# Clamped decay differences as Relu on ScalarE, and a convolution from an SBUF copy, in a hybrid decoder layer

## The chip, the cores and the metric

The kernel runs on one core of one Trainium2 chip. The metric is device time in microseconds (us) from the first to the last instruction of one execution; times of a kernel are the median of several executions. Engines are called by the names of the profile: PE (TensorE matmul) with PEld (its weight loads), DVE (VectorE), ACT (ScalarE), POOL (GpSimd), SP (SyncE, which only issues transfers here). L529 is line 529 of the kernel.

## What is computed

One decoder layer over 1024 tokens of width 1024, float32. One input projection (width 4696) feeds two mixers: group A, a Mamba-2 state-space part (16 heads of 64, two B/C groups of state 128), and group B, a sparse attention in which every query keeps its 256 best keys by a small indexer. Their outputs are projected, added to the input, and normalized; a convolved SwiGLU channel mixer and a second normalization follow. The change touches group A alone, of which this is the core:

```python
xbc = jax.nn.silu(_causal_dwconv(xbc, ssd_conv_w, ssd_conv_b))   # width 4, 1536 channels
xs, bm, cm = jnp.split(xbc, [SSD_INNER, SSD_INNER + SSD_BC], axis=-1)
dt = jax.nn.softplus(dt_raw + dt_bias)
acs = jnp.cumsum((dt * a).reshape(bsz, nc, q, SSD_GROUPS, hg), axis=2)   # in chunks of 128
seg = acs[:, :, :, None] - acs[:, :, None, :]
lmat = jnp.exp(jnp.where(causal[:, :, None, None], seg, -jnp.inf))
y_diag = jnp.einsum("bclsg,bclsgh,bcsghp->bclghp", cb, lmat, xdt)
```

## The kernel before, in words

**Matrix products.** Each float32 operand is split in a high and a low part (`split`, L125 to L130: the low part is a subtraction, on POOL for the weights of this stage), and each product is three matmuls (`three`, L156 to L159). `cols_half` (L161) makes 128 output channels by 512 tokens with 24 matmuls into one PSUM bank of tag "ip", which has two banks. `tok_proj_gen` (L603) makes 128 tokens by 256 columns of the gate z or of v into the same two banks and evicts them on ACT (L617).

**Convolution.** `conv_tile(j)` (L469) makes one of twelve tiles of 128 channels of x (j below 8), B (8, 9) and C (10, 11), tokens along the free axis. It goes by halves of 512 tokens. ACT reads the half from PSUM, scaled by the last tap and with the bias (L479); the other three taps are multiply-adds on DVE that read PSUM shifted (L483). The first three tokens of the second half need the end of the first: ACT keeps three columns in `edge` (L478), and three narrow multiply-adds use them (L486). All of this stands under a raised priority (EV_PRIO). After the second half comes SiLU on ACT (L491, L494), and for x eight transposes on PE and copies on ACT (L500, L502). The tile has a buffer of tag "wo" (8 buffers, shared with the indexer's scores) or "pt" (3).

**Chunked scan.** `ssd_gen(g)` (L512) walks eight chunks of 128 tokens for each of the two groups. Per chunk, SP loads a row of cumulative decays, broadcast over partitions, as `acsb` (L525, 512 KB in SBUF); eight DVE instructions, one per head, make min(row - own decay, 0) over 128x128 (L529); ACT takes the exponential of all eight (L531); DVE multiplies by the masked product of C and B (L535, L536); POOL makes the scaled inputs (L539 to L543). Then PE multiplies with the running state (L548) and makes its increment (L554) and the chunk's output (L564), and DVE adds the increment to the state (L558).

**Order.** SP's queue is in program order. The order on the other engines is set when the kernel is built, by a planner that simulates a time line and takes the ready instruction of highest priority. The program interleaves generators: the indexer's scores (`score_gen`) beside the first projections; then `topk_gen` (a search over 32 bits, with sign passes on ACT at L353, counts on DVE at L350 and some small integer operations such as L358, L364 and L367 after each) beside `main`: convolution tiles 0 to 3, then z, q and `ssd_gen(0)`, then tiles 9, 11, 4 to 7 and the gate of group 0, then z, v, q and `ssd_gen(1)`. `ssd_gen` has a priority of its own (SSD_PRIO) under EV_PRIO. The attention begins at about 640 us, the channel mixer after 1040 us. The channel mixer has a convolution of width 3 whose input lies in SBUF (L1058, L1061); the attention's exponentials are L686.

Of the kernel before, what the change touches and what calls it, by code (L numbers as in the profile page):

```python
# [12 lines left out]
AF = mybir.ActivationFunctionType  # L13
OP = mybir.AluOpType

P = 128
L = 1024
# [40 lines left out]
def hybrid_layer(ctx, tc, x, w_in, ssd_conv_w, ssd_conv_b, dt_bias, a_log, d_skip, ssd_norm_g,  # L58
                 idx_k_norm_g, idx_k_norm_b, w_out, ln1_g, ln1_b, w_up, ffn_conv_w, ffn_conv_b,
                 w_down, ln2_g, ln2_b, out):  # L60
    nc = tc.nc
# [15 lines left out]
    def big(name, dtype=F32, shape=(P, 1024), tag="t4"):  # L77
        return pool.tile(list(shape), dtype, name=name, tag=tag, bufs=BUFS[tag])

    def bank(name, tag, shape=(P, 512)):  # L80
        return psum.tile(list(shape), F32, name=name, tag=tag, bufs=PBUFS[tag])

    def small(name, shape, dtype=F32, bufs=2):
        return pool.tile(list(shape), dtype, name=name, tag=name, bufs=bufs)

    def mid(name, dtype=F32, shape=(P, 512), tag="s2"):
        return pool.tile(list(shape), dtype, name=name, tag=tag, bufs=S2 if tag == "s2" else EV)
# [73 lines left out]
    def cols_half(w, mov, half, tag="ip"):  # L161

        hi, lo, m = w
        ps = bank("proj", tag)
        for k in range(NK):
            three(ps[:m], hi[:, k, :m], lo[:, k, :m], mov[0](half, k), mov[1](half, k), k == 0, k == NK - 1)
        return ps
# [23 lines left out]
    cw = consts.tile([P, 68], F32, name="cw")  # L191
    ps = bank("cwps", "tp")
# [3 lines left out]
    for half in range(2):  # L196
        s = slice(half * 512, half * 512 + 512)
        for k in range(NK):
            ps = bank("xtp", "lg")
# [8 lines left out]
    for half in range(2):  # L208
        ps = cols_half(w_small, xt, half)
        nc.scalar.activation(sg[:88, half * 512:half * 512 + 512], ps[:88], AF.Copy)  # L210
    tok = big("tok", shape=(P, 1024))[:, :NB * 88].rearrange("p (b c) -> p b c", c=88)
    for g in range(2):
        ps = bank("sgp", "tp")
# [21 lines left out]
    for b in range(NB):  # L235
        nc.vector.tensor_scalar(kn[:, b, :64], tok[:, b, 16:80], mv8[:, b, 0:1], rs8[:, b:b + 1],
                                op0=OP.subtract, op1=OP.mult)
# [4 lines left out]
    for g in range(2):  # L242
        s = slice(g * 512, g * 512 + 512)
        ps = bank("kip", "tp")
# [189 lines left out]
    def next_w(ahead=1):  # L434
        load_ahead(1)
        w = ready.pop(0)
        load_ahead(ahead)
        return w
# [3 lines left out]
    for t in range(4):  # L442
        w = w_qi if t == 0 else next_w()
        a, c = big("qsa", F32R, tag="pp"), big("qsb", F32R, tag="pp")
        for half in range(2):
            s = slice(half * 512, half * 512 + 512)
            ps = cols_half(w, xt, half)
# [20 lines left out]

    def conv_tile(j):  # L469
        w = next_w()  # L470
        t = big("conv", tag="wo" if j < 8 else "pt")
        edge = small("edge", (P, 3))
        for half in range(2):
            o = half * 512
            ps = cols_half(w, xt, half)
            with tc.high_priority(EV_PRIO):
                if half == 0:
                    nc.scalar.activation(edge, ps[:, 509:512], AF.Copy)  # L478
                nc.scalar.activation(t[:, o:o + 512], ps, AF.Identity, bias=cw[:, 48 + j:49 + j],  # L479
                                     scale=cw[:, 36 + j:37 + j])  # L480
                for sft in (1, 2, 3):
                    tap = cw[:, (3 - sft) * 12 + j:(3 - sft) * 12 + j + 1]
                    nc.vector.scalar_tensor_tensor(t[:, o + sft:o + 512], ps[:, :512 - sft], tap, t[:, o + sft:o + 512],  # L483
                                                   op0=OP.mult, op1=OP.add)
                    if half == 1:
                        nc.vector.scalar_tensor_tensor(t[:, o:o + sft], edge[:, 3 - sft:], tap, t[:, o:o + sft],  # L486
                                                       op0=OP.mult, op1=OP.add)
            yield
        if j >= 8:
            bc[j] = t  # L490
            nc.scalar.activation(t, t, AF.Silu)  # L491
        else:
            g, jj = divmod(j, 4)
            nc.scalar.activation(t, t, AF.Silu)  # L494
            if jj == 0:
                xs[g] = [big("xs", shape=(P, 2, 512), tag="pp") for _ in range(4)]
            for c4 in range(2):
                ps = bank("xsp", "tp")
                for c in range(4):
                    nc.tensor.transpose(ps[:, c * P:(c + 1) * P], t[:, (c4 * 4 + c) * P:(c4 * 4 + c + 1) * P], ident)  # L500
                for c in range(2):
                    nc.scalar.activation(xs[g][c4 * 2 + c][:, :, jj * P:(jj + 1) * P],  # L502
                                         ps[:, c * 256:c * 256 + 256].rearrange("p (c n) -> p c n", c=2), AF.Copy)


    def heads(ap, g, c):
        return ap[:, c, g * 8:g * 8 + 8][:, :, None].to_broadcast([P, 8, 64])

    def hv(t):
        return t.rearrange("p (h n) -> p h n", h=8)  # L510

    def ssd_gen(g, tag):  # L512
        dt, acs, eacs, cd, dd = decays
        bt, ct = bc[8 + g], bc[10 + g]
        state = None
        for c in range(NB):
            cs = slice(c * P, (c + 1) * P)
            if c % 4 == 0:
                ps = bank("btp", "tp")
                for j in range(4):  # L520
                    nc.tensor.transpose(ps[:, j * P:(j + 1) * P], bt[:, (c + j) * P:(c + j + 1) * P], ident)
                btok = mid("btok", shape=(P, 4, P))
                nc.scalar.activation(btok, ps.rearrange("p (j n) -> p j n", j=4), AF.Copy)
            ab = big("acsb", tag=tag, shape=(P, 8, P))
            nc.sync.dma_start(ab, bass.AP(tensor=a_dr.tensor, offset=a_dr.offset + (c * 16 + g * 8) * P,  # L525
                                          ap=[[0, P], [P, 8], [1, P]]))
            lm = big("lmat", tag=tag, shape=(P, 8, P))
            for h in range(8):
                nc.vector.tensor_scalar(lm[:, h, :], ab[:, h, :], acs[:, c, g * 8 + h:g * 8 + h + 1], 0.0,  # L529
                                        op0=OP.subtract, op1=OP.min)  # L530
            nc.scalar.activation(lm, lm, AF.Exp)  # L531
            ps = bank("cbps", "tp")
            nc.tensor.matmul(ps[:, :P], bt[:, cs], ct[:, cs], start=True, stop=True)
            cb = small("cbm", (P, P))
            nc.vector.tensor_tensor(cb, ps[:, :P], tri, op=OP.mult)  # L535
            nc.vector.tensor_tensor(lm, lm, cb[:, None, :].to_broadcast([P, 8, P]), op=OP.mult)  # L536
            xc = xs[g][c // 2][:, c % 2, :]
            xd = [mid("xdt"), mid("xdd") if c < NB - 1 else None]
            nc.gpsimd.tensor_tensor(hv(xd[0]), hv(xc), heads(dt, g, c), op=OP.mult)  # L539
            if c < NB - 1:  # L540
                nc.gpsimd.tensor_tensor(hv(xd[1]), hv(xc), heads(dd, g, c), op=OP.mult)
            skip = mid("skip")
            nc.gpsimd.tensor_tensor(hv(skip), hv(xc), dsk[:, g * 8:g * 8 + 8][:, :, None].to_broadcast([P, 8, 64]),  # L543
                                    op=OP.mult)
            yield
            if c:
                po = bank("yoff", "lg")
                nc.tensor.matmul(po, ct[:, cs], state, start=True, stop=True)  # L548
                off = mid("off")
                nc.vector.tensor_tensor(hv(off), hv(po), heads(eacs, g, c), op=OP.mult)  # L550
                nc.gpsimd.tensor_tensor(skip, skip, off, op=OP.add)
            if c < NB - 1:
                pst = bank("stps", "lg")
                nc.tensor.matmul(pst, btok[:, c % 4, :], xd[1], start=True, stop=True)  # L554
                new = mid("state")
                if c:
                    nc.gpsimd.tensor_tensor(hv(new), hv(state), heads(cd, g, c), op=OP.mult)
                    nc.vector.tensor_tensor(new, new, pst, op=OP.add)  # L558
                else:
                    nc.vector.tensor_copy(new, pst)  # L560
                state = new
            py = bank("yps", "lg")
            for h in range(8):
                nc.tensor.matmul(py[:, h * 64:h * 64 + 64], lm[:, h, :], xd[0][:, h * 64:h * 64 + 64],  # L564
                                 start=True, stop=True)
            nc.vector.tensor_tensor(xc, py, skip, op=OP.add)
            yield
# [335 lines left out]
    ps = bank("fwps", "tp")  # L903
# [36 lines left out]
    for i, b in enumerate(LN_ORDER):  # L940
        bs = slice(b * P, (b + 1) * P)
        o = (b % 4) * P
# [8 lines left out]
        for n in range(2):  # L951
            ns = slice(n * 512, n * 512 + 512)
            ps = bank("ops", ("ip", "lg")[n])
# [7 lines left out]
        for k4 in range(2):  # L961
            ps = bank("hTp", "tp")
# [69 lines left out]
    for j in range(NF):  # L1032
# [10 lines left out]
        c = bank("pc", "tp")  # L1043
# [13 lines left out]
        for x_, v_, ct in ((xu, vu, NF + j), (xg, vg, j)):  # L1057
            nc.scalar.activation(v_, x_, AF.Identity, bias=fw[:, 132 + ct:133 + ct], scale=fw[:, 88 + ct:89 + ct])  # L1058
            for sft in (1, 2):
                tap = fw[:, (2 - sft) * 44 + ct:(2 - sft) * 44 + ct + 1]  # L1060
# [77 lines left out]
```

## Time and profile before

| | |
|---|---|
| median of three runs | 1767.94 us (1764.98 to 1770.79) |
| the profiled execution's own time | 1762.1 us |
| its span, first to last instruction | 1760.2 us |
| mean granted TensorE clock | 0.972 |
| instructions | 22843 |

The profile is of one execution. Busy time of an engine is the union of its instructions; idle time is told with what ended it. A row of waits says who waited for whom, the time in total, how often, and the longest. The span is the profiled execution's; a time for the change is worked out against it and then set beside the median of the runs.

### The profile page before, as it was taken

To read this page: it belongs to the slowest core of one execution; us is meant where nothing else is said; L and a number is where in the kernel's file an instruction comes from. 1 tells how busy PE (TensorE), PEld (TensorE's weight loads), DVE (VectorE), ACT (ScalarE), POOL (GpSimd) and SP (SyncE) were. 2 spreads that over 40 slices of the span, in tenths; PEclk is the share of its full clock that TensorE was granted. 3 is DMA by queue.
4 is the path that set the end of the run, shared out by engine and by line. 5 is a ranking of instruction groups with operands and counts; after the bars stand their busy time and mean duration, and the time that the engine had idled before them with its cause. 6 is when DMAs were issued, how large, how long until landed. Compare 5 with 4: busy or idle time off the path is not lost.

```text
span 1760.2 us, 22843 instructions
## 1 busy us (share of the span) xinstructions
PE 1622.6 (92%) x7976; PEld 1342.8 (76%) x7976; DVE 1245.4 (71%) x2289; ACT 841.3 (48%) x1495; POOL 803.9 (46%) x560
## 2 busy tenths in 40 slices
PE   7899977888998989999999885999999999899998
PEld 6788866766887767778888764888888888688886
DVE  3534799998689667777787479888788786515516
ACT  3243474676411466666676344444444443333231
POOL 3223224453355443545464357765555553445351
PEclk9999999998999999999999997999999999899999
DMA  5122122123332473545454451322222223446443
GB/s 166 50 67 66 53 64 65 61 78 90 117 96 75 144 216 102 162 133 142 131 160 151 149 171 57 96 85 84 85 84 84 90 74 112 136 147 232 155 147 128
DMA packets 180937, 198.21 MB, mean 113 GB/s; under 512 B 12003, under 2 KB 136279, under 8 KB 180823
## 3 DMA queue, kind: packets, MB, share of 16 engines
q1 hardware_dynamic: 147351, 145.37, 28.0%
q10 hardware_dynamic: 33472, 51.39, 8.0%
q8 instruction: 63, 1.03, 0.3%
q14 instruction: 51, 0.42, 0.1%
HBM read 145.28 MB, written 51.45 MB: 112 GB/s over the span
## 4 chain that ended last, share of the span: by engine, by line
PE 44%; DVE 6%; DMA 2%; ACT 2%; issue 1%; POOL 1%; SPq 0%; DVEq 0%; ACTq 0%; POOLq 0%
PE acc L157 5%; PE acc L158 5%; PE acc L159 4%; PE pc L157 2%; PE pd L157 2%; PE pd L158 2%; PE pc L158 2%; PE pa L157 2%; PE pd L159 2%; PE pc L159 2%; PE ops L158 2%; PE ops L157 2%; PE ops L159 2%; PE pa L158 2%; PE pa L159 2%; PE ptp L695 2%
## 5 line engine op out<-in xcount | busy, mean ns | idle before, releaser
L130 POOL TENSOR_TENSOR w_lo<-w_raw,w_hi 128x1024 fp32r<-128x1024 f32 (+1 forms) x89 | 221.9, 2499 | 162.5 <-ACT w_hi L129 160.2
L157 PE MATMUL proj<-xTh,w_hi 128*128 128x512 f32 (+1 forms) x432 | 175.5, 407 | 30.2 <-DVE conv L483 10.4
L158 PE MATMUL proj<-xTl,w_hi 128*128 128x512 f32 (+1 forms) x432 | 173.7, 402 | 0.0
L159 PE MATMUL proj<-xTh,w_lo 128*128 128x512 f32 (+1 forms) x432 | 172.9, 401 | 0.0
L1003 POOL TENSOR_TENSOR w_hl<-s,w_hl 128x512 fp32r<-128x512 f32 x88 | 129.5, 1476 | 81.2 <-ACT w_hl L1002 80.8
L689 POOL TENSOR_SCALAR prob<-prob,sm 128x512 f32<-128x512 f32 (+7 forms) x128 | 97.5, 772 | 144.6 <-DVE sm L688 114.0
L1081 DVE TENSOR_TENSOR g_hl<-g_raw,g_hl 128x512 fp32r<-128x512 f32 x44 | 59.3, 1354 | 133.7 <-ACT g_hl L1080 129.3
L1003 POOL TENSOR_TENSOR w_hl<-w_raw,w_hl 128x512 fp32r<-128x512 f32 x66 | 106.3, 1613 | 88.9 <-ACT w_hl L1002 58.5
L157 PE MATMUL acc<-w_hi,g_hl 128*128 128x512 f32 x352 | 136.3, 395 | 7.8 <-ACT g_hl L1080 7.8
L158 PE MATMUL acc<-w_lo,g_hl 128*128 128x512 f32 x352 | 137.5, 391 | 0.0
L159 PE MATMUL acc<-w_hi,g_hl 128*128 128x512 f32 x352 | 137.4, 390 | 0.0
L127 POOL TENSOR_SCALAR w_hi<-w_raw 128x1024 fp32r<-128x1024 f32 x35 | 40.8, 1167 | 185.2 <-PE proj L158 153.6
L157 PEld LDWEIGHTS proj<-xTh,w_hi 128*128 128x128 f32 (+1 forms) x432 | 83.5, 193 | 50.6 <-issue 30.5
L686 ACT ACTIVATE prob<-prob,mx 128x512 f32<-128x512 f32 (+7 forms) x128 | 98.5, 771 | 39.2 <-DVE mx L683 36.0
L697 ACT ACTIVATE pt<-ptp 128x512 fp32r<-128x512 f32 x144 | 81.2, 594 | 65.4 <-PE ptp L695 44.6
L698 DVE TENSOR_TENSOR pt<-ptp,pt 128x512 fp32r<-128x512 f32 x144 | 95.5, 685 | 15.5 <-ACT pt L697 15.2
L157 PE MATMUL ops<-w_hi,y_hi 128*128 128x512 f32 x256 | 102.4, 401 | 4.1 <-ACT y_hi L129 3.1
L157 PE MATMUL tps<-w_hi,xTh 128*128 128x256 f32 x320 | 95.9, 301 | 9.6 <-ACT tout L617 6.9
L353 ACT ACTIVATE junk<-score,cand 128x1024 bf16<-128x1024 f32 (+2 forms) x96 | 86.1, 897 | 35.8 <-DVE cand L367 26.1
L158 PE MATMUL ops<-w_lo,y_hi 128*128 128x512 f32 x256 | 101.4, 396 | 0.4 <-DVE w_lo L130 0.4
L159 PE MATMUL ops<-w_hi,y_lo 128*128 128x512 f32 x256 | 100.5, 397 | 0.4 <-POOL y_lo L130 0.4
L129 ACT ACTIVATE w_hi<-w_raw 128x1024 fp32r<-128x1024 f32 (+1 forms) x62 | 65.2, 1052 | 74.0 <-PE acc L159 53.2
(315 smaller groups left out, 4793.3 us busy)
## 6 DMA issues: line engine op xcount, KB each, us to landing
w_raw<-in_ffn_w_up_dram SPq DMA_DIRECT2D x44, 512.0 KB, 3.9
w_raw<-in_ffn_w_down_dram SPq DMA_DIRECT2D x44, 512.0 KB, 3.7
w_raw<-in_w_in_dram SPq DMA_DIRECT2D x36, 512.0 KB, 4.1
r_dr<-rout ACTq DMA_DIRECT2D x48, 256.0 KB, 2.1
g_dr<-vg ACTq DMA_DIRECT2D x22, 512.0 KB, 2.6
g_raw<-g_dr SPq DMA_DIRECT2D x44, 256.0 KB, 4.0
acsb<-a_dr SPq DMA_DIRECT2D x16, 512.0 KB, 4.1
w_raw<-in_w_out_dram SPq DMA_DIRECT2D x16, 512.0 KB, 4.2
```

What stands on the lines that cost most here:

```text
L129: nc.scalar.activation(hi, raw, AF.Copy)
L130: (nc.vector if lo_on_dve else nc.gpsimd).tensor_tensor(lo, raw, f(hi), op=OP.subtract)
L157: nc.tensor.matmul(ps, ah, bh, start=start, stop=False, skip_group_check=onto)
L158: nc.tensor.matmul(ps, ah, bl, start=False, stop=False, skip_group_check=onto)
L159: nc.tensor.matmul(ps, al, bh, start=False, stop=stop, skip_group_check=onto)
L353: nc.scalar.activation(junk[1][:, :n], score_ap[b], AF.Sign, bias=c, scale=-1.0, accum_out=val[e][:, i:i + 1])
L686: nc.scalar.activation(t[:, :w], t[:, :w], AF.Exp, bias=mx[:, h:h + 1], scale=-1.0, accum_out=sm[:, h:h + 1])
L689: nc.gpsimd.tensor_scalar(t[:, :w], t[:, :w], sm[:, 4 + h:5 + h], 1.0, op0=OP.mult, op1=OP.mult)
L697: nc.scalar.activation(pt[:, 0], ps, AF.Copy)
L698: nc.vector.tensor_tensor(pt[:, 1], ps, f(pt[:, 0]), op=OP.subtract)
L1003: nc.gpsimd.tensor_tensor(t[:, 1], src, f(t[:, 0]), op=OP.subtract)
L1081: nc.vector.tensor_tensor(t[:, 1], raw, f(t[:, 0]), op=OP.subtract)
```

## The change

The eight clamped subtractions of a chunk become eight activations: Relu of (own decay - row), with the own decay as a bias per partition; the exponential then gets a scale of -1. The convolution copies each half of the projection from PSUM to a tile `raw` of tag "tx" (three buffers that the channel mixer uses later), and after the second half makes the scaled read on ACT and three taps on DVE over all 1024 tokens from that tile. `edge` and its instructions go. The raised priority holds for the copies alone, and the generator yields once between the halves and once after the taps, as many times as before.

```diff
--- before.py
+++ after.py
@@ -468,24 +468,18 @@
 
     def conv_tile(j):
         w = next_w()
-        t = big("conv", tag="wo" if j < 8 else "pt")
-        edge = small("edge", (P, 3))
+        t, raw = big("conv", tag="wo" if j < 8 else "pt"), big("xbc", tag="tx")
         for half in range(2):
-            o = half * 512
             ps = cols_half(w, xt, half)
             with tc.high_priority(EV_PRIO):
-                if half == 0:
-                    nc.scalar.activation(edge, ps[:, 509:512], AF.Copy)
-                nc.scalar.activation(t[:, o:o + 512], ps, AF.Identity, bias=cw[:, 48 + j:49 + j],
-                                     scale=cw[:, 36 + j:37 + j])
-                for sft in (1, 2, 3):
-                    tap = cw[:, (3 - sft) * 12 + j:(3 - sft) * 12 + j + 1]
-                    nc.vector.scalar_tensor_tensor(t[:, o + sft:o + 512], ps[:, :512 - sft], tap, t[:, o + sft:o + 512],
-                                                   op0=OP.mult, op1=OP.add)
-                    if half == 1:
-                        nc.vector.scalar_tensor_tensor(t[:, o:o + sft], edge[:, 3 - sft:], tap, t[:, o:o + sft],
-                                                       op0=OP.mult, op1=OP.add)
-            yield
+                nc.scalar.activation(raw[:, half * 512:half * 512 + 512], ps, AF.Copy)
+            if half == 0:
+                yield
+        nc.scalar.activation(t, raw, AF.Identity, bias=cw[:, 48 + j:49 + j], scale=cw[:, 36 + j:37 + j])
+        for sft in (1, 2, 3):
+            tap = cw[:, (3 - sft) * 12 + j:(3 - sft) * 12 + j + 1]
+            nc.vector.scalar_tensor_tensor(t[:, sft:], raw[:, :L - sft], tap, t[:, sft:], op0=OP.mult, op1=OP.add)
+        yield
         if j >= 8:
             bc[j] = t
             nc.scalar.activation(t, t, AF.Silu)
@@ -526,9 +520,9 @@
                                           ap=[[0, P], [P, 8], [1, P]]))
             lm = big("lmat", tag=tag, shape=(P, 8, P))
             for h in range(8):
-                nc.vector.tensor_scalar(lm[:, h, :], ab[:, h, :], acs[:, c, g * 8 + h:g * 8 + h + 1], 0.0,
-                                        op0=OP.subtract, op1=OP.min)
-            nc.scalar.activation(lm, lm, AF.Exp)
+                nc.scalar.activation(lm[:, h, :], ab[:, h, :], AF.Relu, bias=acs[:, c, g * 8 + h:g * 8 + h + 1],
+                                     scale=-1.0)
+            nc.scalar.activation(lm, lm, AF.Exp, scale=-1.0)
             ps = bank("cbps", "tp")
             nc.tensor.matmul(ps[:, :P], bt[:, cs], ct[:, cs], start=True, stop=True)
             cb = small("cbm", (P, P))
```

## Rows read from the trace of the kernel before

**Rows 1.** The page of the profile, part 1: busy us, share, instructions, whole execution.
```profile
PE 1622.6 (92%) x7976; PEld 1342.8 (76%) x7976; DVE 1245.4 (71%) x2289; ACT 841.3 (48%) x1495; POOL 803.9 (46%) x560
```

**Rows 2.** Busy time by stretch: us, busy per engine, granted clock, DMA share, GB/s.
```profile
220.00:420.00 200.00, 159.88 (x891) 134.02 (x890) 195.82 (x518) 135.81 (x277) 84.90 (x65) 0.92 0.24 72
420.00:500.00 80.00, 74.38 (x440) 64.45 (x439) 51.95 (x107) 33.31 (x60) 24.25 (x18) 0.96 0.31 100
500.00:600.00 100.00, 86.75 (x591) 77.76 (x589) 95.68 (x142) 18.97 (x33) 60.66 (x38) 0.97 0.31 87
600.00:640.00 40.00, 34.67 (x156) 27.61 (x156) 15.13 (x25) 23.88 (x41) 7.18 (x3) 0.96 0.73 212
```

**Rows 3.** Waits of PE from 160 to 640 us: waiter, releaser, us, times, longest.
```profile
PE yoff L548 <- DVE state L558: 17.8, 7, 7.4
PE proj L157 <- DVE conv L483: 10.4, 2, 6.3
PE proj L157 <- DVE neg L364: 7.2, 1, 7.2
PE tps L157 <- ACT tout L617: 6.9, 4, 3.1
PE tps L158 <- POOL w_lo L130: 3.9, 1, 3.9
```

**Rows 4.** Timeline, 288 to 297 us, POOL, DVE and PE: start, length, what.
```profile
290.90 4.64 POOL L130 TENSOR_TENSOR w_lo<-w_raw,w_hi 128x1024 fp32r<-128x1024 f32 x2
...
288.58 4.74 DVE L529 TENSOR_SCALAR lmat<-acsb,dtset 128x128 f32<-128x128 f32 x4
293.24 2.32 DVE L367 SCALAR_TENSOR_TENSOR cand<-fail,base 128x2 int32<-128x2 int32 x1
...
296.21 1.22 PE L548 MATMUL yoff<-state,conv 128*128 128x512 f32 x1 [7.41 <-DVE state L558]
```

**Rows 5.** Timeline, 385 to 394 us, ACT and PE.
```profile
386.19 0.77 ACT L479 ACTIVATE conv<-proj,cw 128x512 f32<-128x512 f32 x1
386.86 1.14 ACT L353 ACTIVATE junk<-score,cand 128x1024 bf16<-128x1024 f32 x1
...
393.45 0.77 PE L157 MATMUL proj<-xTh,w_hi 128*128 128x512 f32 x1 [6.32 <-DVE conv L483]
```

**Rows 6.** Groups of instructions by line, DVE, 160 to 640 us.
```profile
L529 DVE TENSOR_SCALAR lmat<-acsb,dtset 128x128 f32<-128x128 f32 x128 | 54.7, 491 | 4.4 <-DMA acsb<-a_dr 3.1 <-PE yps L564 1.0 <-PE xsp L500 0.2
L483 DVE SCALAR_TENSOR_TENSOR conv<-proj,cw,conv 128x511 f32<-128x511 f32 (+2 forms) x72 | 53.5, 743 | 23.6 <-ACT conv L479 23.2
...
L486 DVE SCALAR_TENSOR_TENSOR conv<-edge,cw,conv 128x1 f32<-128x1 f32 (+2 forms) x36 | 22.3, 619 | 0.0
```

**Rows 7.** Groups of instructions by line, ACT, 160 to 640 us.
```profile
L479 ACT ACTIVATE conv<-proj,cw 128x512 f32<-128x512 f32 x24 | 18.6, 777 | 9.6 <-PE proj L159 9.6
...
L531 ACT ACTIVATE lmat<-lmat 128x1024 f32<-128x1024 f32 x16 | 16.9, 1058 | 42.8 <-DVE lmat L529 36.5 <-DVE cand L367 6.2
```

**Rows 8.** Single lines of DVE, count: shortest/median/longest ns, first and last start.
```profile
L529 DVE TENSOR_SCALAR lmat<-acsb,dtset x128: 266/276/2441, 220.1 to 571.7; 128x128 f32<-128x128 f32 x128
...
L483 DVE SCALAR_TENSOR_TENSOR conv<-proj,cw,conv x72: 730/742/752, 166.1 to 473.9; 128x511 f32<-128x511 f32 x24, 128x510 f32<-128x510 f32 x24, 128x509 f32<-128x509 f32 x24
...
L1061 DVE SCALAR_TENSOR_TENSOR vg<-xg,fw,vg x44: 1271/1858/2366, 1103.9 to 1505.4; 128x1023 f32<-128x1023 f32 x22, 128x1022 f32<-128x1022 f32 x22
```

**Rows 9.** Groups by line and shape, ACT, whole execution.
```profile
L1058 ACT ACTIVATE vu<-xu,fw 128x1024 f32<-128x1024 f32 x22 | 27.4, 1246 | 17.6 <-DVE xu L1051 15.2 <-DMA g_dr<-vg 1.1
...
L461 ACT ACTIVATE qkout<-proj 128x512 f32<-128x512 f32 x20 | 11.8, 590 | 6.3 <-PE proj L159 6.3
...
L686 ACT ACTIVATE prob<-prob,mx 128x128 f32<-128x128 f32 x16 | 6.2, 393 | 1.6 <-DVE mx L683 1.6
```

**Rows 10.** Waits of the SP queue, 160 to 640 us.
```profile
SPq L525 <- DVE lmat L529: 108.2, 9, 42.8
```

**Rows 11.** Line L308 on ACT: shortest/median/longest ns, first and last start.
```profile
L308 ACT ACTIVATE relu<-sps x80: 417/522/599, 72.0 to 222.4; 128x512 f32<-128x512 f32 x24, 128x384 f32<-128x384 f32 x24, 128x448 f32<-128x448 f32 x16, 128x320 f32<-128x320 f32 x16
```

## The prediction, made before the change was run

> **What bounds the kernel now.** I read the busy shares first: PE is busy 92% of the span, DVE 71%, ACT 48%, POOL 46% [rows 1]. TensorE's work does not change here, so only time in which PE is idle, or granted the slower clock, can be won. The windows show where that is. The change touches work between 160 and 640 us, and PE's idle time lies from 220 on: up to 420 it is idle 40.1 of 200 us while DVE is busy 195.8, from 500 to 600 idle 13.3 while DVE is busy 95.7 of 100; with the 5.6 and 5.3 us of the two other stretches that makes 64.3 us [rows 2]. In those two stretches VectorE is the full engine and ScalarE is not: 135.8 of 200 and 19.0 of 100. The granted clock also falls: lost full-speed time is (1 - 0.92) x 200 + 0.04 x 80 + 0.03 x 100 + 0.04 x 40 = 23.8 us, part of it inside the idle gaps [rows 2].
>
> The waits of PE say who ends the gaps [rows 3]: 17.8 us until the DVE addition that makes the running state, 10.4 us for a PSUM bank that the convolution taps still read, 7.2 us more under a tiny DVE operation (L364) that happened to end last: what PE needs there is again a bank of a convolution tile. I count 17.6 us as the convolution's. 6.9 us wait for ScalarE's eviction of a z block, 3.9 for POOL; 18.1 us are smaller pieces, without rows here.
>
> Two close views show the mechanism. Around 290 us POOL runs two w_lo passes (4.64 us together); four of the decay subtractions, 0.28 us each when alone, take 4.74 us beside them, then a 128x2 operation takes 2.32, and the state that PE waits for comes 7.41 us late [rows 4, 8]. Around 386 us ScalarE reads a convolution half at 386.19, but PE gets the next bank only at 393.45, after a 6.32 us gap: the bank was held until DVE had made the third tap [rows 5].
>
> **Part 1, decay differences.** 128 DVE subtractions go: 54.7 us of DVE, of which 128 x 0.276 = 35 us is their bare work and the rest waiting beside POOL [rows 6, 8]. 128 Relu come on ACT. The nearest row has the same shape and a bias read per partition: 0.393 us [rows 9]. Neighbours on ACT overlap by 0.10 (one starts at 386.19 and lasts 0.77, the next starts at 386.86 [rows 5]), so the step is 0.29 us and 128 take 38 us; the bounds are 37 and 50. Much of it finds ACT idle: the exponentials that follow wait 36.5 us for exactly these subtractions [rows 7]. A chunk's eight take 2.3 us on ACT; on DVE they took 8 x 0.276 = 2.2 when alone and more beside POOL, so the chain from the decay row to the exponential is no longer. Relu comes without a table load in all 80 places where it stands now [rows 11]; I cost loads at nothing, at worst one of 1.28 us per chunk, 16 x 1.28 = 20 us of ACT.
>
> Queues: no DMA is added. SP issues the same 16 decay-row loads, each of which waits for a buffer to be read out (108.2 us on SP, with weight and z loads queued behind) [rows 10]; that release now comes from ACT, and I take it as neither earlier nor later. The new wait is on ACT: a Relu whose row has not landed holds up everything behind it, the evictions of z blocks and convolution halves among it.
>
> **Part 2, convolution.** Per tile, 6 taps and 3 edge taps on DVE become 3 taps over 1024 tokens. Removed: 53.5 + 22.3 = 75.8 us [rows 6]. Added: 36 taps with both tensors in SBUF. The row nearest is the feed-forward convolution, same operation over 1023: 1.27 us at the shortest, 1.86 median, 2.37 longest [rows 8]. I take 1.6, between the shortest and the median, since POOL is busy 85 of 200 us here [rows 2]: 58 us, with bounds 46 and 85. On ACT 24 scaled reads (18.6 us [rows 7]) become 24 plain copies at 0.59 and 12 scaled passes at 1.25 [rows 9]: 14.2 + 15.0 - 18.6 = +10.6 us. The 12 removed edge copies I leave uncounted, they only lower this. The bank is now free after the copy alone; taps and scaled pass read SBUF and lose the raised priority, and nothing on PE waits for them until the tile's transposes.
>
> Row against rule: the 72 taps from PSUM take 730 to 752 ns whatever POOL does, while the SBUF taps of the feed-forward part spread from 1271 to 2366 [rows 8]. The Trainium skill, "SBUF — State Buffer", section "SBUF: two separate sides", says that a VectorE operation with two SBUF inputs and a GpSimd operation exclude each other for a whole instruction. The traces agree, and the rule speaks against this part: it makes immune work exposed. What it would do at its full price is the second rival below.
>
> **Sum.** DVE, 160 to 640 us: -54.7 - 75.8 + 58 = -72 us, of which about 10 is overlap of neighbours. ACT: +38 + 11 = +49; in 220 to 420 half of the Relu (19) and some of the rest bring 135.8 to about 158 of 200. No engine then is full. PE's time:
> - banks held by the taps, 17.6 us: a copy of 0.59 replaces up to 7 us of holding; I leave a fifth: -14.
> - waits for the state, 17.8 us: in the gap above 4.7 of 7.4 us were the moved subtractions, but POOL's passes also stop the small operations that stay (2.32 us there): half: -9.
> - smaller pieces, 18.1: a quarter, those of convolution banks: -4.
> - evictions on ACT wait behind Relu batches: 6.9 grows to about 12: +5.
> - clock: after the long gaps that go PE does not fall to the slower level: a third of 23.8: -8.
>
> Together -30 us: 1762.1 for the profiled execution becomes 1732. That execution lies 5.8 us (0.3%) under the median of the runs, 1767.9; at the median the forecast is **1738 us**. All else follows 640 us; with PE busy 92% of the span [rows 1] a shift at 640 should reach the end, but the chain of waits itself does not reach back into this stretch, which is a reason for doubt.
>
> **Rivals.** All times at the median.
> - More is won: every gap with a DVE releaser goes. -17.6 - 17.8 - 10 of the smaller ones, and -14 of clock, is -59: 1709 us. For it: DVE is full only there. Against: POOL's passes remain. Chance 0.10.
> - The lock takes the relief: taps at 2.37 us make 85 us, more than the 75.8 removed, and the operations that remain stand behind the same w_lo passes that the subtractions stood behind, so the state waits stay; or time won is waited away at 640. Left are the -14 of the banks and perhaps -4 of clock, less 5 for ACT, at best -13: 1755, at worst nothing, 1768. For it: the 2.32 us in [rows 4]. Against: DVE had no slack and now has 60 us. Chance 0.28.
> - Slower: ScalarE's one queue becomes what PE waits for. A batch of eight Relu and its exponential is 2.3 + 1.06 us in one piece; a z-block eviction behind it frees its bank late. The longest such stall today is 3.1 us [rows 3]; one per chunk, 16 x 3.1 = 50 us, minus the -35 won elsewhere, is +15: 1783 us. It decides from where PE's waits for ACT reach about 42 us. For it: topk's sign passes already fill ACT to 135.8 of 200. Against: evictions have raised priority, and ACT waits much for DVE now. Chance 0.12.
>
> The Trainium skill, "ScalarE: Activation LUTs", section "Rules for kernel authors", says that relu, max and min belong on VectorE, which is faster per element. By the rows the moved operation does take 0.39 instead of 0.28 us. It would make the change a loss only where ScalarE is the fuller engine, the last rival.
>
> **Numbers.** The forecast case, 1718 to 1755, has 0.50. A measurement here can tell about 0.3% (5 us) from no change. Faster by more: 0.50 + 0.10 + two thirds of the second rival, 0.18 = 0.78; same: the rest of it, 0.10; slower 0.12. The range is 1712 to 1770: below it lies half of the first rival (0.05), above it the slower case and a little of "same" (0.15).
>
> **What would show it.** Right: DVE's busy time from 220 to 640, 359 us in the four stretches [rows 2], falls by some 50 (the rest of the relief lies before 220), PE's waits on convolution banks fall under 5 us, the state waits halve, PE reaches the first attention units some 30 us earlier, Relu is about 0.39 us, taps about 1.6. Wrong: taps near 2.4 us or state waits unchanged (the lock); z-block evictions as the longest wait of PE (the queue); table loads beside the Relu; or PE early at 640 us and late again after it.

## The result, and the profile after

The change makes the kernel faster by a little over one per cent: median 1745.11 us (four runs, 1741.8 to 1747.83) against 1766.46 us for the kernel before (four runs, 1763.92 to 1770.79). The ratio is 0.9886, 95% interval 0.987 to 0.9902; that is 20 us, where 30 were forecast. The profiled execution took 1747.83 us (span 1745.8), the slowest of the four, against 1762.1, which is below all four timed runs of the kernel before: 14.3 us less. Traces are compared below with that difference in mind.

The page of the profile after, part 1, which answers to [rows 1]: VectorE has 52.5 us less, ScalarE 48.0 more, TensorE as much as before.

```profile
PE 1624.8 (93%) x7976; PEld 1346.9 (77%) x7976; DVE 1192.9 (68%) x2089; ACT 889.3 (51%) x1625; POOL 801.3 (46%) x560
```

The same four windows as [rows 2], after (us, busy time of each engine, granted clock, DMA share, GB/s):

```profile
220.00:420.00 200.00, 173.60 (x965) 146.34 (x964) 185.22 (x427) 160.73 (x345) 93.05 (x68) 0.95 0.26 78
420.00:500.00 80.00, 77.41 (x519) 69.59 (x518) 38.53 (x57) 52.44 (x115) 33.81 (x25) 0.98 0.38 120
500.00:600.00 100.00, 88.22 (x541) 76.46 (x540) 72.89 (x112) 28.88 (x63) 43.91 (x30) 0.95 0.35 105
600.00:640.00 40.00, 29.01 (x124) 21.63 (x123) 26.90 (x72) 29.44 (x59) 16.57 (x12) 0.83 0.72 208
```

Up to 500 us this is the forecast: PE idle 26.4 us of 200 instead of 40.1, then 2.6 of 80 instead of 5.6, at a higher clock (0.95 and 0.98 for 0.92 and 0.96). From 500 on nothing is won: PE is idle 11.8 of 100 (13.3 before) and 11.0 of the last 40, twice the 5.3 of before, and the clock there is 0.83 instead of 0.96. In all PE's idle time fell from 64.3 to 51.8 us. Lost full-speed time, counted as in the prediction, is 10 + 1.6 + 5 + 6.8 = 23.4 us against 23.8: the slower level has not gone, it has moved behind 500 us.

PE's waits from 160 to 620 us, after (waiter, releaser, us, times, longest), as in [rows 3]:

```profile
PE yT L588 <- DVE xs L582: 11.9, 3, 6.6
PE yoff L542 <- DVE state L552: 10.0, 4, 4.5
PE proj L157 <- POOL w_hi L127: 6.6, 1, 6.6
...
PE proj L157 <- ACT qkout L461: 3.7, 2, 3.1
...
PE tps L157 <- ACT tout L611: 2.1, 1, 2.1
PE proj L157 <- ACT xbc L475: 1.7, 2, 1.0
PE tps L157 <- ACT xbc L475: 1.6, 1, 1.6
```

The bank waits that were counted as 17.6 us are 1.7 + 1.6 under the copy `xbc`. The state waits fell from 17.8 to 10.0. The z-block evictions fell too (6.9 to 2.1). New at the top are the gate's transposes (L588; 11.9, where the kernel before had 2.0) and one wait of 6.6 us for a weight.

The costs of the parts, first DVE groups from 160 to 640 us, after (name, count, busy us and mean ns, idle before and its releaser), beside [rows 6]:

```profile
L481 DVE SCALAR_TENSOR_TENSOR conv<-xbc,cw,conv 128x1023 f32<-128x1023 f32 (+2 forms) x36 | 53.8, 1496 | 24.0 <-ACT conv L478 23.6
...
L367 DVE SCALAR_TENSOR_TENSOR cand<-fail,base 128x2 int32<-128x2 int32 (+1 forms) x60 | 23.6, 401 | 0.7
...
L358 DVE TENSOR_SCALAR base<-cand 128x2 int32<-128x2 int32 (+1 forms) x60 | 20.0, 345 | 0.0
```

and the ACT groups of the same stretch, beside [rows 7]:

```profile
L523 ACT ACTIVATE lmat<-acsb,dtset 128x128 f32<-128x128 f32 x128 | 39.5, 389 | 24.5 <-PE yps L558 12.6 <-DMA acsb<-a_dr 11.9
...
L478 ACT ACTIVATE conv<-xbc,cw 128x1024 f32<-128x1024 f32 x12 | 14.8, 1236 | 0.1
L475 ACT ACTIVATE xbc<-proj 128x512 f32<-128x512 f32 x24 | 14.1, 588 | 6.2 <-PE proj L159 5.7 <-ACT qkout L590 0.4
```

Relu is 0.389 us, the taps 1.5 us on average, the copies and scaled passes as priced. The Relu now have 24.5 us of idle time before them, where the exponentials had 42.8.

**Where PE lost its lead.** The first attention logits start where PE has finished this part. The last of the 40 z and v evictions and those logits, before (operation, count, shortest/median/longest ns, first and last start, one fence per kernel):

```profile
L617 ACT ACTIVATE tout<-tps x40: 359/372/400, 251.6 to 590.9; 128x256 f32<-128x256 f32 x40
...
L680 PEld LDWEIGHTS lgps<-kh,qst x192: 186/188/192, 635.6 to 969.7; 128*128 128x128 f32 x192
```

and after:

```profile
L611 ACT ACTIVATE tout<-tps x40: 360/384/402, 250.0 to 553.1; 128x256 f32<-128x256 f32 x40
...
L674 PEld LDWEIGHTS lgps<-kh,qst x192: 186/188/337, 620.4 to 952.9; 128*128 128x128 f32 x192
```

The last eviction is 37.8 us earlier; the same matmuls compared one by one are about 25 us early near 420 (times of the kernel before), 27 near 537 and 37 near 571. The first logits are only 15.2 us earlier. So more than the forecast 30 us was there at 570, and more than half of it was given back by 620. The timeline of that stretch, after (start, length, engine and line; in brackets the idle time before and its releaser):

```profile
572.43 3.56 SPq L569 DMA_DIRECT2D zs<-z_dr  x2
...
576.15 0.38 SPq L138 DMA_DIRECT2D w_raw<-in_w_in_dram  x1
580.08 10.24 SPq L569 DMA_DIRECT2D zs<-z_dr  x6
581.00 1.20 POOL L127 TENSOR_SCALAR w_hi<-w_raw 128x1024 fp32r<-128x1024 f32 x1 [5.36 <-DMA w_raw<-in_w_in_dram]
...
582.25 0.80 PE L157 MATMUL proj<-xTh,w_hi 128*128 128x512 f32 x1 [6.56 <-POOL w_hi L127]
...
608.06 0.48 PE L588 MATMUL yT<-ident,xs 128*128 128x128 f32 x1 [6.60 <-DVE xs L582]
```

and the waits of SP's queue from 480 to 640 us, after:

```profile
SPq L569 <- DVE mask L410: 13.6, 1, 13.6
SPq L569 <- ACT sq L574: 11.3, 5, 3.5
```

SP issues in program order. (Its longest waits in this stretch are others, 24.6 us for a decay row and 21.4 for a weight; both end before 535 us, and PE has no gap for a weight there.) The second group's gate needs eight loads of z (L569). Their tiles are of one small set of buffers that also holds the scan's own tiles and the marks `eq` of the search (L383), so the first load waits 13.6 us, until the mask (L410) has read such marks, and the second for a tile of the scan. The last weight load of the stage stands behind these two: it is issued at 576.15, and PE waits 6.56 us for the weight. The other six z loads are issued from 580.08 on, so the gate ends late: the scan ends at 579.8, the gate's transposes start at 608.06, 28 us later, after another gap of 6.60 us. From 590 to 603 us the gate also stands in ACT's own queue, behind evictions of projections that PE ends late after its wait for that weight (ACT is idle 5.11 and 1.33 us before them, DVE 7.50 and 3.75 for the z blocks that ACT makes behind them). The windows with these two gaps are those with the lower clock.

### The profile page after: what moved, and what is told of

Its sections match the earlier page's. It is cut to its first block, busy times and chain, and to the rows that moved or that the text cites. A ratio compares the mean times of both kernels' runs of the same rounds, so it can differ in the third digit from the quotient of the medians.

```text
span 1745.8 us, 22765 instructions
## 1 busy us (share of the span) xinstructions
PE 1624.8 (93%) x7976; PEld 1346.9 (77%) x7976; DVE 1192.9 (68%) x2089; ACT 889.3 (51%) x1625; POOL 801.3 (46%) x560
## 4 chain that ended last, share of the span: by engine, by line
PE 50%; DVE 8%; issue 2%; ACT 2%; DMA 2%; POOL 0%; ACTq 0%; DVEq 0%; POOLq 0%; SPq 0%
PE acc L157 5%; PE acc L159 5%; PE acc L158 5%; PE ops L157 3%; PE ops L158 3%; PE ops L159 3%; PE ptp L689 3%; PE pc L157 2%; PE pc L158 2%; PE pc L159 2%; PE pa L157 2%; PE pd L158 2%; PE pd L157 2%; PE pd L159 2%; PE pa L158 2%
## 5 line engine op out<-in xcount | busy, mean ns | idle before, releaser
L159 PE MATMUL acc<-w_hi,g_hl 128*128 128x512 f32 x352 | 137.6, 391 | 0.0
L691 ACT ACTIVATE pt<-ptp 128x512 fp32r<-128x512 f32 x144 | 81.1, 594 | 64.3 <-PE ptp L689 43.7
L692 DVE TENSOR_TENSOR pt<-ptp,pt 128x512 fp32r<-128x512 f32 x144 | 95.5, 684 | 15.6 <-ACT pt L691 15.2
```

The lines of the kernel that those rows point to most:

```text
L159: nc.tensor.matmul(ps, al, bh, start=False, stop=stop, skip_group_check=onto)
L691: nc.scalar.activation(pt[:, 0], ps, AF.Copy)
L692: nc.vector.tensor_tensor(pt[:, 1], ps, f(pt[:, 0]), op=OP.subtract)
```

## The experiments

Each of the twelve kernels was timed beside the kernel before. Savings in us are (1 - ratio) x 1765. The planner orders all engines anew for every kernel, so an edit never changes one thing alone; for that reason the same edit was tried on several kernels.

**Each part by itself.** Only the Relu:

```diff
-                nc.vector.tensor_scalar(lm[:, h, :], ab[:, h, :], acs[:, c, g * 8 + h:g * 8 + h + 1], 0.0,
-                                        op0=OP.subtract, op1=OP.min)
-            nc.scalar.activation(lm, lm, AF.Exp)
+                nc.scalar.activation(lm[:, h, :], ab[:, h, :], AF.Relu, bias=acs[:, c, g * 8 + h:g * 8 + h + 1],
+                                     scale=-1.0)
+            nc.scalar.activation(lm, lm, AF.Exp, scale=-1.0)
```

> The decay differences as Relu on ACT alone; the convolution as before. Theory: both parts free PE, so Relu alone gives about half of the change's 21 us: 8 to 14 us under the kernel before; the waits for the running state fall from 19 to about 10 us, the banks held by the taps stay (17 us). Rival (the lock): the convolution from SBUF costs what it wins, so Relu alone is as fast as the whole change or faster, 20 us or more under the kernel before.

Measured 1762.12 us, ratio 0.9982 [0.9969, 0.9995]: 3 us, less than either theory. The waits of PE, 160 to 640 us, of that kernel show that the state waits did fall, from 17.8 to 13.3, and that the taps still hold the banks, about half of it under small operations that ended last:

```profile
PE yoff L548 <- DVE state L558: 13.3, 5, 6.6
PE tps L157 <- DVE conv L483: 5.1, 1, 5.1
PE proj L157 <- DVE cand L365: 5.0, 1, 5.0
PE proj L157 <- DVE cand L367: 4.6, 1, 4.6
...
PE tps L157 <- DVE conv L486: 4.2, 1, 4.2
```

Only the convolution:

```diff
-                nc.scalar.activation(t[:, o:o + 512], ps, AF.Identity, bias=cw[:, 48 + j:49 + j],
-                                     scale=cw[:, 36 + j:37 + j])
...
+                nc.scalar.activation(raw[:, half * 512:half * 512 + 512], ps, AF.Copy)
...
+            nc.vector.scalar_tensor_tensor(t[:, sft:], raw[:, :L - sft], tap, t[:, sft:], op0=OP.mult, op1=OP.add)
```

> The convolution from the SBUF copy alone; the decay differences on DVE as before. Theory: the bank waits (17 us) go, the state waits stay: 6 to 13 us under the kernel before. Rival (the lock): taps wait beside POOL and DVE stays full, 0 to 10 us over the kernel before.

Measured 1767.23 us, ratio 1.0017 [1.0006, 1.0028]: 3 us slower (1 to 5). The number is the rival's; its mechanism is tested further down, with SP's queue freed. For the bank waits are gone here as well (3.6 + 0.6 us under the copy), and PE was 21 us ahead near 571. By the first logits it was 10 us behind the kernel before (645.9 against 635.6). Its waits:

```profile
PE yoff L542 <- DVE state L552: 14.0, 5, 7.0
...
PE yoff L542 <- DVE fail L360: 7.1, 1, 7.1
...
PE proj L157 <- POOL w_hi L127: 5.7, 1, 5.7
...
PE proj L157 <- ACT xbc L475: 3.6, 2, 2.4
```

The state comes late 14.0 + 7.1 us here (the 7.1 is a state wait too, under a small operation that ended last). The last weight of the stage is issued at 597.41 here, where it was 590.09 before and 576.15 after. So a lead was won and lost, and the savings of the two parts, 3 and -3, do not add up to 20. That called for a theory of what stands at the end: SP's queue.

**SP's queue freed, on the kernel after.** First the z and the k loads in buffers of tag "tx", which neither scan nor search uses:

```diff
-            zs = mid("zs")
+            zs = big("zs", shape=(P, 512), tag="tx") if g else mid("zs")
...
-            kr = big("kraw", tag="wr")
+            kr = big("kraw", tag="tx")
```

> The changed kernel, with the buffers of the k loads and of the second group's z loads taken from the three that the convolution copy has left free, so that these loads don't wait in SP's queue ahead of decay rows and weights. Theory: what was ahead by 30 us or more near 570 us was given back because SP's queue stood still; 6 to 15 us under the changed kernel, the 6.6 us wait of PE for w_hi near 582 us and ACT's 10 us wait for a decay row near 545 us gone. Rival: the lead is lost to the gate's own chain (scaling, transposes), whatever SP does; within 3 us of the changed kernel.

Measured 1739.73 us, ratio 0.9846 [0.9829, 0.9862]: 27 us under before, 7 under the kernel after. The wait for the weight is gone. Then the z loads alone:

```diff
-            zs = mid("zs")
+            zs = big("zs", shape=(P, 512), tag="tx") if g else mid("zs")
```

> The changed kernel with only the z loads of the second group in the three buffers that the convolution copy left free; the k loads where they were. Theory: the z loads are the stop of SP's queue that costs most, 6 to 14 us under the changed kernel. Rival: only k and z loads together matter; within 4 us of the changed kernel.

Measured 1738.36 us, ratio 0.9837 [0.982, 0.9855]: 29 us under before, 9 under after. The z loads are what mattered. The last weight is issued at 555.29, 21 us earlier than after, and the gate's transposes start 6 us after the scan's end (584.9 against 578.8) instead of 28.

**The k loads put off** by five steps of the planner's program (`KDEL`, L34), which leaves the z loads in the shared buffers; on the kernel after, on the one before, and on the convolution alone, the same line each time:

```diff
-KDEL = 11
+KDEL = 16
```

> The changed kernel with the attention's k loads issued five steps later, so that every decay row of the second group stands ahead of them in SP's queue. Theory: SP stands at the k loads (their buffers come free only with topk's masks), a row lands 10 us late on ACT, the second group's scan stretches and the lead is lost with it; the scan ends near 566 instead of 580 us, 5 to 15 us under the changed kernel. Rival: the scan is held by DVE's mask work itself; its end moves by under 4 us and the time stays within 3 us of the changed kernel's.

Measured 1747.9 us, ratio 0.9901 [0.9882, 0.992]: no gain on the kernel after, though the scan ended at 572.2 instead of 579.8. So the theory failed; of the rival the time held, and what it said of the scan's end did not. The last weight is issued at 571.46, only 5 us earlier, and the transposes followed at 602.6, still 30 us behind: the scan's end is not what the gate waits for while the z loads are late.

> The kernel before the change with the same later k loads. Theory: DVE is full from 500 to 600 us there, SP is not what the scan waits for most; 0 to 5 us under the kernel before. Rival: the order of the k loads costs every kernel the same 5 to 15 us and has nothing to do with the change.

Measured 1767.39 us, ratio 1.0008 [0.9998, 1.0017]: nothing.

> The convolution part alone with the later k loads. Theory: this part leads by 12 to 21 us near 560 us and loses all of it before 640; with SP freed some stays: 5 to 12 us under the kernel before. Rival: the lead is lost to DVE, full with the decay differences until 600 us: no change against the convolution part alone, 0 to 6 us over the kernel before.

Measured 1761.79 us, ratio 0.9973 [0.9959, 0.9987]: 5 us under before, 8 better than the convolution alone, just short of the expectation.

**Both edits** (`KDEL = 20` and the z loads in "tx"), on all four kernels: after, before, convolution alone, Relu alone.

```diff
-KDEL = 11
+KDEL = 20
...
-            zs = mid("zs")
+            zs = big("zs", shape=(P, 512), tag="tx") if g else mid("zs")
```

> The changed kernel with the k loads behind all decay rows and the last weights, and the second group's z loads in the three free buffers of the convolution copy. Theory: the two stops of SP's queue add up: 12 to 22 us under the changed kernel, the best of all. Rival: one bound takes the other's place (k comes late for the attention): 0 to 6 us under the kernel with the two buffers changed.

Measured 1731.52 us, ratio 0.9805 [0.9789, 0.982]: 34 us under before, 14 under after, the fastest of all kernels here. SP's timeline of this kernel shows the last weight of the stage issued at 521.95, 54 us earlier than after, and the last z load out by 542:

```profile
507.34 1.17 SPq L569 DMA_DIRECT2D zs<-z_dr  x2
521.95 0.38 SPq L138 DMA_DIRECT2D w_raw<-in_w_in_dram  x1
522.43 19.57 SPq L569 DMA_DIRECT2D zs<-z_dr  x6
```

Its last two windows have the clock at 0.98 and 0.96 again:

```profile
500.00:600.00 100.00, 90.98 (x556) 78.27 (x554) 85.30 (x126) 40.14 (x77) 48.30 (x31) 0.98 0.46 137
600.00:640.00 40.00, 33.93 (x175) 26.11 (x174) 26.78 (x82) 29.43 (x61) 20.02 (x19) 0.96 0.65 190
```

and its landmarks are

```profile
L611 ACT ACTIVATE tout<-tps x40: 357/370/401, 248.6 to 551.3; 128x256 f32<-128x256 f32 x40
...
L674 PEld LDWEIGHTS lgps<-kh,qst x192: 186/188/266, 600.9 to 938.9; 128*128 128x128 f32 x192
```

The projections are as early as in the kernel after (551.3 and 553.1), but the first logits are 34.7 us earlier than before instead of 15.2, and the last ones (938.9 against 969.7) still 30.8. What PE waits for from 160 to 640 us in this kernel is now led by evictions on ACT:

```profile
PE proj L157 <- ACT qkout L461: 6.8, 2, 3.8
PE yoff L542 <- DVE state L552: 6.7, 5, 2.5
PE tps L157 <- ACT tout L611: 6.5, 4, 3.1
```

> The kernel before with both freeings of SP's queue (k loads behind the last weights, second group's z loads in three unused buffers). Theory: there PE waits for DVE all through this stretch, SP costs little: 0 to 8 us under the kernel before. Rival: the stop costs every kernel the 14 us that it costs the changed one: 11 to 17 us under the kernel before.

Measured 1766.88 us, ratio 1.0009 [0.9995, 1.0023]: nothing. The first logits are 9.7 us earlier than before (625.9), the last ones 3.0 later (972.7): early first logits alone are not yet a gain. A free queue by itself is worth nothing; it only keeps what the change wins.

> The convolution part alone with both freeings. Theory: its lead of 12 to 21 us near 560 us now mostly stays: 8 to 18 us under the kernel before. Rival: DVE, still full with the decay differences, takes the lead back: 0 to 6 us under it.

Measured 1748.08 us, ratio 0.9891 [0.9875, 0.9907]: 19 us, where the convolution alone had none. VectorE still makes the decay differences here, and the taps read the SBUF copy, so neither the rival of this run nor that of the convolution alone is what took the lead there.

> The Relu part alone with both freeings. Theory: its lead of 7 to 12 us near 560 us stays, 6 to 14 us under the kernel before. Rival: the banks held by the taps limit it and the freeings do nothing: 0 to 5 us under it.

Measured 1758.55 us, ratio 0.9956 [0.994, 0.9973]: 8 us.

Together these kernels form a square (us saved against before):

| | neither part | Relu | convolution | both |
|---|---|---|---|---|
| SP's queue as it was | 0 | 3 | -3 | 20 |
| z loads in "tx", k loads later | -2 | 8 | 19 | 34 |

With the queue freed the sum of the parts, 27, comes near the 34 of both. With the queue as it was, the parts alone are lost at the end.

The traces say how. In the ten kernels without both edits, the one before and the one after among them, the last weight of the stage is issued anywhere from 555 to 598 us, and the first logits follow it by 42 to 49 us each time (45.5 before, 44.3 after). In the four kernels with both edits the weight goes out between 522 and 552 us, and the logits follow 74 to 83 us later: there something else sets them. This is a pattern over kernels whose orders differ, not a test of its own.

**The load on ScalarE.** In the kernel after, each Relu issued twice, the same result written again:

```diff
-                nc.scalar.activation(lm[:, h, :], ab[:, h, :], AF.Relu, bias=acs[:, c, g * 8 + h:g * 8 + h + 1],
-                                     scale=-1.0)
+                for _ in range(2):
+                    nc.scalar.activation(lm[:, h, :], ab[:, h, :], AF.Relu, bias=acs[:, c, g * 8 + h:g * 8 + h + 1],
+                                         scale=-1.0)
```

> The changed kernel with each Relu made twice into the same place: 128 more on ACT, about 38 us of its time. Theory: ACT has idle time enough, 0 to 8 us over the changed kernel. Rival (ACT's one queue is what PE waits for next): 15 to 40 us over it, with waits of PE for evictions as the longest.

Measured 1755.64 us, ratio 0.9936 [0.9921, 0.9951]: 9 us over the kernel after, for 40 us more on ACT, by its group of instructions:

```profile
L524 ACT ACTIVATE lmat<-acsb,dtset 128x128 f32<-128x128 f32 x256 | 79.3, 392 | 13.5 <-DMA acsb<-a_dr 7.8 <-PE yps L559 5.5
```

So about three quarters of the added time is hidden: 9 / 40 = 0.22 us are paid per us added, in an order that the planner made anew. It is a little more than the theory had and well under its rival. PE's lead at 420 us was not touched; what it lost against the kernel after it lost from about 465 us on, in the second scan.

## Why the prediction was mostly right

The sign, the order of size and the mechanism up to 570 us held; 1745.1 lies in the forecast case, 7 us above its centre, and of the 30 us forecast 20 came. The sum, term by term (us; "freed" is the kernel after with both edits to SP's queue; waits from 160 us on):

| term | predicted | after | freed |
|---|---|---|---|
| banks held by taps, of 17.6 | -14 | -14.3 | -14.3 |
| state waits, of 17.8 | -9 | -7.8 | -11.1 |
| z-block evictions on ACT, of 6.9 | +5 | -4.8 | -0.4 |
| PE idle, 220 to 640 | -22 | -12.5 | -19.4 |
| clock, of 23.8, as the prediction counts it | -8 | -0.4 | -10.6 |
| profiled execution | -30 | -14.3 | -29.6 |

**What held.** Relu took 39.5 us of ACT (38 predicted), with the idle time of the exponentials gone (0.1 us instead of 42.8, of which 36.5 for the subtractions [rows 7]; 24.5 now lie before the Relu) and no table load before it. The taps took 53.8 us (58 predicted, bounds 46 to 85). A copy does free the bank: 3.3 us of waits, under the 5 named. ACT's evictions were to cost 5 us more and cost less: `tout` fell by 4.8, `qkout` rose from 2.5 to 3.7. With the queue freed the two are 6.5 + 6.8 = 13.3 us where they were 9.4 before, so the term comes back once PE is not held elsewhere. The rival of the slower ScalarE needed 42 us of waits for ACT; in the kernel after there are about 12.

**VectorE's relief was smaller than forecast.** Its busy time from 220 to 640 us fell from 358.6 to 323.5, 35 us and not 50. Most of the difference is work moved in: up to 600 us it fell by 47, and from 600 to 640 it rose by 12 (72 instructions instead of 25), since the attention begins earlier. Over the whole execution it fell by 52.5 us, where the sum had 72 less 10 of overlap. What is missing there is, as far as the rows show, waiting beside POOL: the subtractions took it with them only in part, and operations that stay meet more of it. Two lines of the search, before (160 to 640 us, as in [rows 6]):

```profile
L367 DVE SCALAR_TENSOR_TENSOR cand<-fail,base 128x2 int32<-128x2 int32 (+1 forms) x60 | 17.9, 307 | 0.4
L358 DVE TENSOR_SCALAR base<-cand 128x2 int32<-128x2 int32 (+1 forms) x60 | 15.9, 280 | 0.0
```

Together they rose from 33.8 to 43.6 us. Others went either way: the accumulation of the scores (L312) rose from 19.2 to 24.3, a comparison of the search (L360) fell from 18.7 to 15.7. This timeline after shows how they wait; the POOL passes over 128x1024 take 2.8 us each in the pair, or 3.33 us alone, and beside them two taps take 5.61, an operation on 128x4 elements 2.33 and another 1.47:

```profile
398.00 5.61 DVE L481 SCALAR_TENSOR_TENSOR conv<-xbc,cw,conv 128x1023 f32<-128x1023 f32 x2
...
399.20 3.33 POOL L130 TENSOR_TENSOR w_lo<-w_raw,w_hi 128x1024 fp32r<-128x1024 f32 x1
...
405.50 5.65 POOL L130 TENSOR_TENSOR w_lo<-w_raw,w_hi 128x1024 fp32r<-128x1024 f32 x2
...
406.52 2.33 DVE L367 SCALAR_TENSOR_TENSOR cand<-fail,base 128x4 int32<-128x4 int32 x1
...
409.70 1.47 DVE L358 TENSOR_SCALAR base<-cand 128x4 int32<-128x4 int32 x1
...
412.49 0.48 PE L588 MATMUL yT<-ident,xs 128*128 128x128 f32 x1 [4.81 <-DVE xs L582]
```

PE's gap of 4.81 us at 412.49 follows on these, though no run here isolates it. Taps and small operations that read SBUF twice wait for POOL; so the second rival's mechanism is there, with one tap at 3.247 us, beyond the 2.37 of its bound. But most taps are short (median 1.282), so it did not take the relief. This is how the Trainium skill, "SBUF — State Buffer", section "SBUF: two separate sides", has it: a VectorE operation with two SBUF inputs and a GpSimd operation exclude each other. The trace agrees for the taps and L367. But L358 reads one tensor and waits as well, 1.47 us where it takes 0.16 alone, as the subtractions did in [rows 4], so the rule as told here covers only a part of what waits.

**The step that failed** is the one on the queue: the release of SP's buffers taken as "neither earlier nor later", with "a shift at 640 should reach the end". SP's k, z and weight loads were costed at nothing, by reading that the queue waited 108.2 us for the subtractions [rows 10] and asking only when these would end. (The prediction has each of the 16 decay-row loads wait for that; the row counts 9 waits.) What else stands in the queue, and in which buffers, was not asked, though the next line of that view of before is a wait of the z loads for the scan:

```profile
SPq L575 <- DVE xs L566: 45.3, 3, 35.4
```

With the projections 30 us earlier, the z loads that wait for buffers of the scan and the search, and the weight behind them, became what PE waits for. That is the half of the second rival in which time won "is waited away at 640"; it was a part, 14 of 34 us by the kernel with both edits, and not the whole.

**The clock term** (-8) was not won by the changed kernel, and in the freed one it is smaller than its own count says. In the kernel after it is -0.4 by the prediction's own count, since the gaps at 582 and 608 came with a mean granted clock of 0.95 and 0.83 in the last two stretches, between the full 2.4 and the slower 1.2 GHz; the first matmul after the gap at 582 takes 0.80 us, where the same at full clock takes 0.39. With the queue freed the weight's gap and the one before the transposes are gone (the largest left near 582 is 3.77 us, for an eviction) and the count gives -10.6. But this count charges the clock for idle time too, in which nothing runs slower, so it can't be added to the idle term. What the clock costs shows in PE's busy time, as the matmuls are the same (their ends are modelled); with the queue freed, the whole execution has

```profile
PE 1617.1 (93%) x7976; PEld 1340.3 (77%) x7976; DVE 1194.0 (69%) x2089; ACT 891.4 (52%) x1627; POOL 803.7 (46%) x560
```

where before had 1622.6 [rows 1] and after 1624.8: 5.5 us less and 2.2 more. The rest of each span is PE's idle time, 137.6 us before, 121.0 after and 113.7 freed. So the 29.4 us by which the freed span is shorter are 23.9 of idle time and 5.5 of busy time, and the 14.4 after are 16.6 less 2.2. The sum had 22 and 8: the freed kernel comes near both, the changed one gets three quarters of the first and nothing of the second. The forecast of 30 was thus that of a kernel whose queue lets the lead through.

**Parts that need each other.** The prediction added the parts up. At the end of this stage two chains meet: PE's stream of projections, which the convolution part speeds up as long as its weights come, and scan, gate and transposes, which VectorE and the z loads set. The first logits need both. By the landmarks, the convolution alone is 14 us ahead in its projections near 601 and loses this behind a wait of 5.7 us for the last weight: the last one ends no earlier than before (622.5 against 623.0; with the queue freed 610.0), and its scan ends later (599.7 against 597.4); the Relu alone ends the scan 4.2 us earlier (593.2), and only both together bring it to 579.8. That both parts are needed is measured; that it is these two chains is read from the traces, and the planner's new order in each kernel is an alternative that these runs can't shut out.

The Trainium skill, "ScalarE: Activation LUTs", section "Rules for kernel authors", which would keep relu on VectorE, has the single operation right (0.389 against 0.276 us) and this kernel wrong: with the queue freed the moved operation wins 8 us by itself and 34 - 19 = 15 beside the convolution.

## What to carry to other kernels

A lead won on the bounding engine must be followed to the next place where chains meet; list there what stands in each in-order issue queue, in which buffers, and who frees them, before a shift is counted to the end. A tile that is loaded for a later stage should not share buffers with the work whose end it waits for, if other loads queue behind it. And a part that shows nothing alone can still be worth its full price: try it beside the other part, and with the next bound out of the way, before it is dropped.

## What the runs showed of the hardware

An operation on 128x4 elements can last nearly as long as a POOL pass over 128x1024 beside it: 2.33 us at 406.52 beside passes of 2.8 us, where the median of that line is 0.16 us. So moving large operations off VectorE took only a part of the waiting off; the operations that came next met the rest. On ScalarE, 128 more activations of 0.39 us, 40 us of an engine busy 160.7 of 200 us at its fullest, cost only 9 us.
